# Four FFN ends of a streaming encoder step: the last six inner tiles joined into one output chain, and a final norm in two halves of the tokens

## The chip, the cores and the metric

The program runs on one core of a Trainium2 chip. The metric is the time of one execution on the device in microseconds (us), and a kernel's time is the median of its runs. A product below is one matmul instruction of TensorE on a 128 x 128 weight block and 288 columns, unless said otherwise.

## What is computed

One inference step of a two-layer encoder (each layer: FFN, mixer of MLA and RWKV heads, cross-attention, FFN), on 512 new frames of one stream and 64 of another, 576 tokens in all, with D_MODEL 1024 and D_FF 2816. The change touches the four FFNs and the final norm:

```python
def rmsnorm(x, g):
    xf = x.astype(jnp.float32)
    y = xf * lax.rsqrt(jnp.mean(xf * xf, axis=-1, keepdims=True) + EPS)
    return (y * g.astype(jnp.float32)).astype(x.dtype)

def swiglu_half(x, g, w_gate, w_up, w_down):
    h = rmsnorm(x, g)
    return x + 0.5 * ((jax.nn.silu(h @ w_gate) * (h @ w_up)) @ w_down)
...
    x = swiglu_half(x, lp['ffn1_norm'], lp['ffn1_w_gate'], lp['ffn1_w_up'], lp['ffn1_w_down'])
    y, c_kv, k_r, wkv, shift = token_mixer(rmsnorm(x, lp['mix_norm']), ...)
    x = x + y
    x = mem_attend(x, mk, mv, lp)
    x = swiglu_half(x, lp['ffn2_norm'], lp['ffn2_w_gate'], lp['ffn2_w_up'], lp['ffn2_w_down'])
...
    y_prompt = rmsnorm(xp, final_norm)
    y_sample = rmsnorm(xs, final_norm)
```

The outputs are y of both streams and the updated caches and states.

## The kernel before

**Layout.** x stays in SBUF for the whole step, as eight tiles x[0..7] of 128 features by 576 tokens. The tokens are worked on in two halves of 288 (`hs`, HT). Every operand of a product is held as two parts, a high part and a low part in fp32r, and one weight block times one activation half is three products: high by high (line L315), low activation (L316), low weight (L317), all in `mm3`. The parts are made by `split`: ScalarE copies the high part (L247), VectorE subtracts it (L248). Weights come by DMA from the SP queue into wraw or sraw buffers and are split into whi/wlo or sh/sl buffers, 128 x 512 (four blocks) at a time, a few ahead of their use (`take`, `factors`).

**An FFN** (`ffn`). The 22 inner tiles are eleven pairs. Pairs 0 and 1 are computed plainly. For pairs 2 to 10 the gate and the up of two tiles by two halves are formed by seven products of sums in place of eight (`products`, `sums`): each gate or up is 84 product instructions. The up result is multiplied by the gate, split, and put into the tags xnh and xnl, rings of eight buffers each (`up`). `outputs` multiplies the inner tiles of one or two pairs with the down weights: for each x tile and half, one accumulator takes all products of the tiles, and VectorE adds half of it into x (L521). The loop over pairs 2 to 10 runs up of pair p, gate of pair p+1, and after pairs 3, 5, 7 and 9 the outputs of the last two pairs (wds weights, 192 products). After pair 10 its outputs alone remain (wd weights, 96 products). The list `order` in `ffn` names the weight blocks in the order of use.

**The next norm** (`Norm`) is made while the outputs end. For every x tile ScalarE makes the high part of gain times x (L370), VectorE the low part (L371), again in the xnh and xnl rings; ScalarE squares the tile (L376) and VectorE adds it to a running sum nacc (L378). The first products of the next stage read the high and low parts without the norm's factor. The factor comes later from one fp32 matmul a half on the sum (L386), which is four instructions (passes) in the trace, and `rsqrt`: three ScalarE steps (L300) and two VectorE corrections (L349, L350).

**The final norm** (`final`). Behind the last FFN's second four output tiles, for each half: eight squares on ScalarE, of which two pairs are added for the whole width beforehand, six fp32 matmuls with the ones matrix in one accumulator (L1411, twelve passes for each half), `rsqrt`, then eight scalings, six on VectorE (L1415) and two on GpSimd (L1417), and four DMAs of y (L1419). The first half's norm stands behind the first halves of x[4..7], the second half's behind the second halves.

**What sets the order.** A scheduler puts the instructions of each engine in one queue when the program is built, and the buffers of a tag are taken in turn: an instruction that writes a buffer waits until the last reader of what stood in it is done. Each engine runs its queue in order.

Of the kernel before, what the change touches and what calls it, by code (L numbers as in the profile page):

```python
# [132 lines left out]
def build(tc, I, O):  # L133
# [266 lines left out]
    def ffn(l, which, V, aside=iter(()), final=None, given=()):  # L400
# [28 lines left out]
        for p in pairs:  # L429
# [3 lines left out]
            if (p - PLAIN) % 2:  # L433
                order += [[wds[l, (p - PLAIN) // 2, m]] for m in range(4)]
        order += [[wd[l, PLAIN, g]] for g in range(2)]
# [93 lines left out]


# [66 lines left out]
        def up(g):  # L597
            acts = [(st([128, T], "xnh", F32R), st([128, T], "xnl", F32R)) for f in range(2)]
# [20 lines left out]
        for p in pairs:  # L619
# [3 lines left out]
            acts += up(g)  # L623
            if not end:
                g = gate()
            if (p - PLAIN) % 2:
                all_outputs(acts)
                acts = []
        if final is None:
            all_outputs(acts)  # L630
        else:
            all_outputs(acts, range(4))
            half_done, done = final()
            outputs(acts, range(4, 8), half_done)
            done()
# [753 lines left out]
    def final():  # L1389

        r, sq = st([128, T], "rstd"), st([128, T], "rs")
        y, qs = ([st([128, 2, HT], "s") for _ in range(8)] for _ in range(2))
        qs = [t.rearrange("p a b -> p (a b)") for t in qs]
        for k in range(4):
            ACT.activation(out=qs[k], in_=x[k], func=AF.Square)
            if k % 2:
                (DVE if k == 1 else POOL).tensor_tensor(out=qs[k], in0=qs[k - 1], in1=qs[k], op=ALU.add)

        def out(k, a):
            return y[2 * (k // 2) + a][:, k % 2]  # L1400

        for k in range(2):
            for a in range(2):
                ACT.activation(out=out(k, a), in_=x[k][:, hs[a]], func=AF.Copy, scale=V("fin", k))

        def tail(a):
            ss, s = ps1("b")[:, 0:HT], hs[a]
            for k in (1, 3, 4, 6, 5, 7):
                if k > 3:
                    ACT.activation(out=qs[k][:, s], in_=x[k][:, s], func=AF.Square)  # L1410
                PE.matmul(ss, ones, qs[k][:, s], start=k == 1, stop=k == 7)  # L1411
            rsqrt(ss, 1.0 / D, EPS, r[:, s], sq[:, s])
            for k in (0, 4, 5, 1, 6, 7, 2, 3):
                if k > 1:
                    DVE.scalar_tensor_tensor(out=out(k, a), in0=x[k][:, s], scalar=V("fin", k), in1=r[:, s], op0=ALU.mult, op1=ALU.mult)  # L1415
                else:
                    POOL.tensor_tensor(out=out(k, a), in0=out(k, a), in1=r[:, s], op=ALU.mult)  # L1417
                if k % 2:
# [109 lines left out]
```

## Time and profile before

| | before |
|---|---|
| median of 3 runs | 2820.01 us (2819.73 to 2820.59) |
| profiled execution | 2819.02 us, its span 2817.0 us |
| granted TensorE clock, mean over the span | 0.991 of full speed |
| TensorE matmul | 2733.7 us, 97% |
| TensorE weight load (beside it) | 2629.8 us, 93% |
| VectorE | 2124.5 us, 75% |
| ScalarE | 1351.2 us, 48% |
| GpSimd | 100.1 us, 4% |

The four places at which an FFN ends lie at about 397 to 425 us (first FFN of layer 0, the mixer follows), 1393 to 1419 (second FFN of layer 0, the first FFN of layer 1 follows), 1791 to 1823 (the mixer follows) and 2786 to 2817 (the final norm follows). The profile's page gives each engine's busy time and a chain of waits, which is followed back from the last instruction. The timeline of an engine gives each instruction with its start, and in brackets the idle time of the engine just before it and the instruction whose end released it. In names, b and mm and g are accumulators (PSUM), xnh and xnl the high and low parts, whi/sh and wlo/sl the high and low parts of weights.

### The profile page before, as it was taken

The numbers are of one execution on the slowest core, as the hardware profiler recorded it, in microseconds if no ns is written. First come the engines' busy times: TensorE is split into PE (matmuls) and PEld (weight loads), VectorE is DVE, ScalarE is ACT, GpSimd is POOL, SyncE is SP. The second block draws the span as 40 slices with busy tenths as digits, with TensorE's granted clock in tenths as the row PEclk, the third lists the DMA queues.
The fourth block names the chain that finished last, engine by engine and source line by source line (L and its number), as shares of the span: only waits on it lengthen the run. The fifth ranks groups of instructions, "written<-read, shape, count | busy, mean of one in ns | idle before, by whom it ended". The sixth has DMA issues, their size and how long they took to land.

```text
span 2817.0 us, 55885 instructions
## 1 busy us (share of the span) xinstructions
PE 2733.7 (97%) x22284; PEld 2629.8 (93%) x22284; DVE 2124.5 (75%) x4356; ACT 1351.2 (48%) x2781; POOL 100.1 (4%) x197
## 2 busy tenths in 40 slices
PE   8999999979999999999999999998999999999998
PEld 8999999968889899999999999997888899999998
DVE  8888876875676678777788777769666765887776
ACT  5544446355544544444444444554555445444443
POOL 0000001010000000000000000012000000000000
PEclk9999999989999999999999999999999999999999
DMA  5333333652233222222223222346433332222221
GB/s 192 101 111 114 112 124 110 158 142 91 92 119 117 72 97 72 92 93 92 94 71 105 91 90 91 109 105 171 118 98 123 98 117 64 91 91 90 92 93 60
DMA packets 187573, 293.21 MB, mean 104 GB/s; under 512 B 87066, under 2 KB 113050, under 8 KB 187138
## 3 DMA queue, kind: packets, MB, share of 16 engines
q1 hardware_dynamic: 185010, 285.46, 32.3%
q0 software_dynamic: 2304, 4.20, 0.6%
q8 instruction: 175, 2.87, 0.4%
q14 instruction: 84, 0.69, 0.1%
HBM read 250.36 MB, written 41.63 MB: 104 GB/s over the span
## 4 chain that ended last, share of the span: by engine, by line
PE 92%; DVE 4%; ACT 2%; issue 1%; DMA 0%; DVEq 0%; SPq 0%; POOL 0%; ACTq 0%
PE b L315 18%; PE b L316 18%; PE b L317 18%; PE mm L315 4%; PE mm L316 4%; PE mm L317 4%; PE g L315 4%; PE g L316 3%; PE g L317 3%; PE sm L1028 2%; PE pp L1028 2%; PE sc L315 2%; PE pp L1052 1%; PE sc L316 1%; PE sc L317 1%; PE tp L981 1%
## 5 line engine op out<-in xcount | busy, mean ns | idle before, releaser
L247 ACT ACTIVATE whi<-wraw 128x512 fp32r<-128x512 f32 (+1 forms) x493 | 305.4, 623 | 543.5 <-PE b L316 264.9
L248 DVE TENSOR_TENSOR wlo<-wraw,whi 128x512 fp32r<-128x512 f32 (+1 forms) x493 | 333.8, 680 | 117.6 <-ACT whi L247 99.9
L317 PE MATMUL b<-s,wlo 128*128 128x288 f32 x1388 | 408.0, 295 | 0.0
L316 PE MATMUL b<-s,whi 128*128 128x288 f32 x1388 | 406.7, 294 | 0.0
L315 PE MATMUL b<-s,whi 128*128 128x288 f32 x1388 | 405.5, 296 | 0.0
L315 PE MATMUL b<-xnh,whi 128*128 128x288 f32 x1168 | 344.5, 298 | 11.5 <-ACT xnh L370 7.6
L316 PE MATMUL b<-xnl,whi 128*128 128x288 f32 x1168 | 346.2, 297 | 3.4 <-DVE xnl L248 1.8
L317 PE MATMUL b<-xnh,wlo 128*128 128x288 f32 x1168 | 343.6, 296 | 0.0
L521 DVE SCALAR_TENSOR_TENSOR x<-b,x 128x288 f32<-128x288 f32 x448 | 196.8, 455 | 132.0 <-PE b L317 131.7
L316 PEld LDWEIGHTS b<-s,whi 128*128 128x128 f32 x1388 | 261.2, 188 | 0.0
L317 PEld LDWEIGHTS b<-s,wlo 128*128 128x128 f32 x1388 | 261.2, 188 | 0.0
L315 PEld LDWEIGHTS b<-s,whi 128*128 128x128 f32 x1388 | 259.5, 188 | 0.0
L315 PEld LDWEIGHTS b<-xnh,whi 128*128 128x128 f32 x1168 | 219.5, 189 | 13.1 <-ACT xnh L370 7.6
L316 PEld LDWEIGHTS b<-xnl,whi 128*128 128x128 f32 x1168 | 220.3, 189 | 5.7 <-DVE xnl L371 2.9
L316 PE MATMUL b<-s,sh 128*128 128x288 f32 x756 | 224.1, 297 | 0.0
L317 PE MATMUL b<-s,sl 128*128 128x288 f32 x756 | 223.1, 296 | 0.0
L315 PE MATMUL b<-s,sh 128*128 128x288 f32 x756 | 223.0, 296 | 0.0
L317 PEld LDWEIGHTS b<-xnh,wlo 128*128 128x128 f32 x1168 | 220.3, 189 | 0.0
L315 PE MATMUL mm<-xnh,whi 128*128 128x288 f32 x688 | 204.2, 298 | 5.2 <-DVE shp L391 1.8
L316 PE MATMUL mm<-xnl,whi 128*128 128x288 f32 x688 | 205.1, 298 | 1.0 <-DVE xnl L371 0.9
L317 PE MATMUL mm<-xnh,wlo 128*128 128x288 f32 x688 | 204.1, 297 | 0.0
L247 ACT ACTIVATE whi<-S 128x512 fp32r<-128x512 f32 x171 | 107.9, 631 | 165.8 <-PE b L316 161.9
(474 smaller groups left out, 7241.4 us busy)
## 6 DMA issues: line engine op xcount, KB each, us to landing
wraw<-in_wgu SPq DMA_DIRECT2D x131, 512.0 KB
wraw<-in_wds SPq DMA_DIRECT2D x48, 512.0 KB
sraw<-in_wgu SPq DMA_DIRECT2D x45, 512.0 KB
wraw<-in_win SPq DMA_DIRECT2D x36, 512.0 KB
wraw<-in_wd SPq DMA_DIRECT2D x21, 512.0 KB
sraw<-in_wds SPq DMA_DIRECT2D x16, 512.0 KB
wraw<-in_wmk SPq DMA_DIRECT2D x16, 512.0 KB
wraw<-in_wmv SPq DMA_DIRECT2D x16, 512.0 KB
```

The source lines that it names most:

```text
L247: ACT.activation(out=h, in_=src, func=AF.Copy)
L248: by.tensor_tensor(out=lo, in0=src, in1=h.bitcast(F32), op=ALU.subtract)
L315: PE.matmul(out, wh, ah, start=first, stop=False, **kw)
L316: PE.matmul(out, wh, al, start=False, stop=False, **kw)
L317: return PE.matmul(out, wl, ah, start=False, stop=last, **kw)
L521: DVE.scalar_tensor_tensor(out=o, in0=p, scalar=0.5, in1=o, op0=ALU.mult, op1=ALU.add)
L981: PE.transpose(pT[0:n, c0:c0 + nq], pe_[e][0:nq, kt * 128:kt * 128 + n], ident[0:nq, 0:nq])
L1028: PE.matmul(o, *f(p4, e), start=(n == 0 and p4 == 0), stop=(n == len(terms) - 1), skip_group_check=True)
L1052: i = PE.matmul(p[:, p4], bk[half(e), p4], ck[half(e), p4, 0:128], start=True, stop=True)
```

## The change

In every FFN the outputs after pair 9 and those after pair 10 become one block after pair 10, `last_outputs`, run for x[0..3] and x[4..7]. For each x tile and half one accumulator takes 4 x 3 products of pairs 8 and 9 and then 2 x 3 of pair 10: 18 products a chain, sixteen chains. Sixteen additions into x remain where there were 32. The order of the weights follows. The up of pair 8 writes into the tags rr, a and rs in place of xnh and xnl; so eight buffers of xnh and xnl hold pairs 9 and 10, and the next norm takes its buffers from another place of the ring: its tiles 4 to 7 use buffers that pairs 9 and 10 stood in, where before its tiles 6 and 7 used those of pair 10.

In the final norm each half squares its own 288 columns, VectorE adds the first seven squares one on another (L1427 of the new file), and the ones matrix is multiplied with that sum and with the eighth square: two fp32 matmuls, four passes. The first half's matmul is put behind the last product of the chain of x[5], second half. GpSimd is not used: VectorE scales, two tiles at a time for the first four (L1438, 128 x 576) and one at a time for the rest (L1441).

The diff, whole:

```diff
@@ -430,9 +430,10 @@
             order += [[wgu[l, 2 * q + r, i] for r in range(2)] for q, i in [(p, 0)] * (p == PLAIN) + [(p, 1)] + [(p + 1, 0)] * (p + 1 < NF // 2)]
             if p == PLAIN:
                 order[-2:-2] = [[wd[l, p - 1, g]] for g in range(2)]
-            if (p - PLAIN) % 2:
+            if (p - PLAIN) % 2 and p < NF // 2 - 2:
                 order += [[wds[l, (p - PLAIN) // 2, m]] for m in range(4)]
-        order += [[wd[l, PLAIN, g]] for g in range(2)]
+        for g in range(2):
+            order += [[wd[l, PLAIN, g]]] + [[wds[l, (NF // 2 - 2 - PLAIN) // 2, 2 * g + m]] for m in range(2)]
 
         def factors():
 
@@ -526,6 +527,31 @@
             per = 4 // len(acts)
             for m in ms[::per]:
                 outputs(acts, range(m, m + per))
+
+        def last_outputs(g, acts, by_halves=None):
+
+            w2 = [take(0 if by_halves else 2) for _ in range(2)]
+            w4 = []
+
+            def some(i, s):
+                p = ps1("b")[:, 0:HT]
+                for f in range(4):
+                    mm3(p, cols(w4[i], f), [t[:, s] for t in acts[f]], f == 0, False)
+                for f in range(2):
+                    end = mm3(p, cols(w2[i // 2], i % 2 * 2 + f), [t[:, s] for t in acts[4 + f]], False, f == 1)
+                o = x[4 * g + i][:, s]
+                DVE.scalar_tensor_tensor(out=o, in0=p, scalar=0.5, in1=o, op0=ALU.mult, op1=ALU.add)
+                return end
+
+            for i in range(4):
+                w4.append(take(0 if by_halves else (2, 2, 2, 1)[i]))
+                for s in hs[0:1] if by_halves else hs:
+                    some(i, s)
+            if by_halves:
+                for i in range(4):
+                    end = some(i, hs[1])
+                    if i == 1:
+                        by_halves(end)
 
 
         def plain(act):
@@ -594,8 +620,8 @@
                 silu(out=g[f][:, e], in_=t, func=AF.Silu)
             return g
 
-        def up(g):
-            acts = [(st([128, T], "xnh", F32R), st([128, T], "xnl", F32R)) for f in range(2)]
+        def up(g, tags=None):
+            acts = [tuple(st([128, T], t or turn(*tags), F32R) for t in (("xnh", "xnl") if tags is None else (None, None))) for f in range(2)]
             for f, e, t in sums(xs, lambda f, e: tmp()):
                 o = t if f + e else tmp()
                 DVE.tensor_tensor(out=o, in0=t, in1=g[f][:, e], op=ALU.mult)
@@ -620,18 +646,19 @@
             end = p == pairs[-1]
             if (p - PLAIN) % 2 == 0:
                 next(aside, None)
-            acts += up(g)
+
+            acts += up(g, ("rr", "a", "rs") if p == NF // 2 - 3 else None)
             if not end:
                 g = gate()
-            if (p - PLAIN) % 2:
+            if (p - PLAIN) % 2 and p < NF // 2 - 2:
                 all_outputs(acts)
                 acts = []
+        last_outputs(0, acts)
         if final is None:
-            all_outputs(acts)
+            last_outputs(1, acts)
         else:
-            all_outputs(acts, range(4))
             half_done, done = final()
-            outputs(acts, range(4, 8), half_done)
+            last_outputs(1, acts, half_done)
             done()
         ps.close()
         sc.close()
@@ -1389,35 +1416,31 @@
     def final():
 
         r, sq = st([128, T], "rstd"), st([128, T], "rs")
-        y, qs = ([st([128, 2, HT], "s") for _ in range(8)] for _ in range(2))
-        qs = [t.rearrange("p a b -> p (a b)") for t in qs]
-        for k in range(4):
-            ACT.activation(out=qs[k], in_=x[k], func=AF.Square)
-            if k % 2:
-                (DVE if k == 1 else POOL).tensor_tensor(out=qs[k], in0=qs[k - 1], in1=qs[k], op=ALU.add)
-
-        def out(k, a):
-            return y[2 * (k // 2) + a][:, k % 2]
-
-        for k in range(2):
-            for a in range(2):
-                ACT.activation(out=out(k, a), in_=x[k][:, hs[a]], func=AF.Copy, scale=V("fin", k))
-
-        def tail(a):
+        y = [st([128, 2, HT], "s") for _ in range(8)]
+
+        def tail(a, prior=None):
             ss, s = ps1("b")[:, 0:HT], hs[a]
-            for k in (1, 3, 4, 6, 5, 7):
-                if k > 3:
-                    ACT.activation(out=qs[k][:, s], in_=x[k][:, s], func=AF.Square)
-                PE.matmul(ss, ones, qs[k][:, s], start=k == 1, stop=k == 7)
+            qs = [st([128, 2, HT], "s")[:, 0] for _ in range(8)]
+            for k in range(8):
+                ACT.activation(out=qs[k], in_=x[k][:, s], func=AF.Square)
+                if 0 < k < 7:
+                    DVE.tensor_tensor(out=qs[k], in0=qs[k - 1], in1=qs[k], op=ALU.add)
+            i = PE.matmul(ss, ones, qs[6], start=True, stop=False)
+            if prior is not None:
+                after(i, prior)
+            PE.matmul(ss, ones, qs[7], start=False, stop=True)
             rsqrt(ss, 1.0 / D, EPS, r[:, s], sq[:, s])
-            for k in (0, 4, 5, 1, 6, 7, 2, 3):
-                if k > 1:
-                    DVE.scalar_tensor_tensor(out=out(k, a), in0=x[k][:, s], scalar=V("fin", k), in1=r[:, s], op0=ALU.mult, op1=ALU.mult)
+            for j in range(4):
+                t = y[2 * j + a]
+                if j < 2:
+                    for i in range(2):
+                        ACT.activation(out=t[:, i], in_=x[2 * j + i][:, s], func=AF.Copy, scale=V("fin", 2 * j + i))
+                    DVE.tensor_tensor(out=t, in0=t, in1=r[:, s].unsqueeze(1).to_broadcast([128, 2, HT]), op=ALU.mult)
                 else:
-                    POOL.tensor_tensor(out=out(k, a), in0=out(k, a), in1=r[:, s], op=ALU.mult)
-                if k % 2:
-                    SP.dma_start(O["y"][k - 1:k + 1, :, s].rearrange("k p t -> p k t"), y[2 * (k // 2) + a])
-        return [lambda a=a: tail(a) for a in range(2)]
+                    for i in range(2):
+                        DVE.scalar_tensor_tensor(out=t[:, i], in0=x[2 * j + i][:, s], scalar=V("fin", 2 * j + i), in1=r[:, s], op0=ALU.mult, op1=ALU.mult)
+                SP.dma_start(O["y"][2 * j:2 * j + 2, :, s].rearrange("k p t -> p k t"), t)
+        return [lambda prior=None, a=a: tail(a, prior) for a in range(2)]
 
     xn = open_xn()
     load_x()
```

TensorE's order at the end of the second FFN. In the kernel before, s_13385 and s_13636 are operands of the last up (pair 10), and its result is xnh_17396 to xnl_17399, which the chains that follow read first:

```order
L315 MATMUL b_17465<-s_13385,whi_17440 128x288
L316 MATMUL b_17465<-s_13385,whi_17440 128x288
L317 MATMUL b_17465<-s_13385,wlo_17441 128x288
L315 MATMUL b_17465<-s_13636,whi_17440 128x288
L316 MATMUL b_17465<-s_13636,whi_17440 128x288
L317 MATMUL b_17465<-s_13636,wlo_17441 128x288
L315 MATMUL b_17547<-xnh_17396,whi_17461 128x288
L316 MATMUL b_17547<-xnl_17397,whi_17461 128x288
L317 MATMUL b_17547<-xnh_17396,wlo_17462 128x288
```

In the changed kernel rr_16500 to rs_16503 are the result of pair 8, xnh_16800 to xnl_16803 that of pair 9, and xnh_17100 and xnl_17101 a tile of pair 10:

```order
L316 MATMUL b_17169<-s_13604,sh_17144 128x288
L317 MATMUL b_17169<-s_13604,sl_17145 128x288
L316 MATMUL b_17257<-a_16501,whi_17209 128x288
L317 MATMUL b_17257<-rr_16500,wlo_17210 128x288
L315 MATMUL b_17257<-a_16502,whi_17209 128x288
L316 MATMUL b_17257<-rs_16503,whi_17209 128x288
L317 MATMUL b_17257<-a_16502,wlo_17210 128x288
L315 MATMUL b_17257<-xnh_16800,whi_17209 128x288
...
L317 MATMUL b_17257<-xnh_16802,wlo_17210 128x288
L315 MATMUL b_17257<-xnh_17100,whi_17165 128x288
L316 MATMUL b_17257<-xnl_17101,whi_17165 128x288
L317 MATMUL b_17257<-xnh_17100,wlo_17166 128x288
```

Between the last up product and the first reader of pair 10 the products of pairs 8 and 9 now stand; the first of these chains (b_17257) reads pair 10 as its last six.

VectorE's order where the second FFN ends and the next norm is made: L521 (before) and L543 (changed) are additions into x, L371 low parts, L378 the sum of squares, L248 weight splits. In the kernel before, the last x tile is x_10368:

```order
L371 SCALAR_TENSOR_TENSOR xnl_17700<-x_10362,narrow_62,xnh_17699 128x576
L521 SCALAR_TENSOR_TENSOR x_10368<-b_17659,x_10368 128x288
L521 SCALAR_TENSOR_TENSOR x_10368<-b_17667,x_10368 128x288
L378 TENSOR_TENSOR nacc_17715<-nacc_17715,nsq_17723 128x576
L371 SCALAR_TENSOR_TENSOR xnl_17704<-x_10364,narrow_62,xnh_17703 128x576
L248 TENSOR_TENSOR sl_17839<-wraw_17836,sh_17838 128x512
L248 TENSOR_TENSOR sl_17867<-wraw_17836,sh_17866 128x512
L371 SCALAR_TENSOR_TENSOR xnl_17708<-x_10366,narrow_62,xnh_17707 128x576
L378 TENSOR_TENSOR nacc_17715<-nacc_17715,nsq_17726 128x576
L371 SCALAR_TENSOR_TENSOR xnl_17712<-x_10368,narrow_62,xnh_17711 128x576
L378 TENSOR_TENSOR nacc_17715<-nacc_17715,nsq_17729 128x576
L378 TENSOR_TENSOR nacc_17715<-nacc_17715,nsq_17732 128x576
```

In the changed kernel the last x tile is x_10336, and x_10330 is the fifth (tile 4):

```order
L543 SCALAR_TENSOR_TENSOR x_10334<-b_17551,x_10334 128x288
L378 TENSOR_TENSOR nacc_17651<-nacc_17651,nsq_17668 128x576
L543 SCALAR_TENSOR_TENSOR x_10336<-b_17571,x_10336 128x288
L371 SCALAR_TENSOR_TENSOR xnl_17636<-x_10330,narrow_62,xnh_17635 128x576
L543 SCALAR_TENSOR_TENSOR x_10336<-b_17591,x_10336 128x288
L371 SCALAR_TENSOR_TENSOR xnl_17640<-x_10332,narrow_62,xnh_17639 128x576
L248 TENSOR_TENSOR sl_17775<-wraw_17772,sh_17774 128x512
L248 TENSOR_TENSOR sl_17803<-wraw_17772,sh_17802 128x512
L371 SCALAR_TENSOR_TENSOR xnl_17644<-x_10334,narrow_62,xnh_17643 128x576
L248 TENSOR_TENSOR wlo_17717<-wraw_17686,whi_17716 128x512
L371 SCALAR_TENSOR_TENSOR xnl_17648<-x_10336,narrow_62,xnh_17647 128x576
L378 TENSOR_TENSOR nacc_17651<-nacc_17651,nsq_17671 128x576
```

Before, three low parts (tiles 5 to 7) and four sums stood behind the last addition; now four low parts (tiles 4 to 7), the first ahead of it, and one sum.

VectorE's order at the very end. In the kernel before, x_27842 is the last x tile; the two corrections and six scalings of the first half stand behind the last addition:

```order
L521 SCALAR_TENSOR_TENSOR x_27840<-b_35190,x_27840 128x288
L521 SCALAR_TENSOR_TENSOR x_27842<-b_35198,x_27842 128x288
L349 SCALAR_TENSOR_TENSOR rs_35086<-b_35145,rs_35086 128x288
L350 SCALAR_TENSOR_TENSOR rstd_35085<-rs_35086,rstd_35085 128x288
L1415 SCALAR_TENSOR_TENSOR s_35091<-x_27836,narrow_62,rstd_35085 128x288
...
L1415 SCALAR_TENSOR_TENSOR s_35089<-x_27834,narrow_62,rstd_35085 128x288
L349 SCALAR_TENSOR_TENSOR rs_35086<-b_35206,rs_35086 128x288
L350 SCALAR_TENSOR_TENSOR rstd_35085<-rs_35086,rstd_35085 128x288
```

In the changed kernel x_27746 is the last x tile, and s_35078 to s_35083 are the running sum of the second half's squares:

```order
L543 SCALAR_TENSOR_TENSOR x_27744<-b_35036,x_27744 128x288
L349 SCALAR_TENSOR_TENSOR rs_34838<-b_34991,rs_34838 128x288
L350 SCALAR_TENSOR_TENSOR rstd_34837<-rs_34838,rstd_34837 128x288
L1438 TENSOR_TENSOR s_34839<-s_34839,rstd_34837 128x576
L1438 TENSOR_TENSOR s_34841<-s_34841,rstd_34837 128x576
L1441 SCALAR_TENSOR_TENSOR s_34843<-x_27740,narrow_62,rstd_34837 128x288
...
L543 SCALAR_TENSOR_TENSOR x_27746<-b_35056,x_27746 128x288
L1427 TENSOR_TENSOR s_35078<-s_35077,s_35078 128x288
...
L1427 TENSOR_TENSOR s_35083<-s_35082,s_35083 128x288
L349 SCALAR_TENSOR_TENSOR rs_34838<-b_35076,rs_34838 128x288
L350 SCALAR_TENSOR_TENSOR rstd_34837<-rs_34838,rstd_34837 128x288
```

The first half's corrections and its six scalings moved ahead of the last addition, and six additions of squares stand behind it.

## Rows read from the trace of the kernel before

**Rows 1.** The page's chain of waits, share of the span by engine

```profile
PE 92%; DVE 4%; ACT 2%; issue 1%; DMA 0%; DVEq 0%; SPq 0%; POOL 0%; ACTq 0%
```

**Rows 2.** Windows: stretch, length, busy time (instructions) of each engine, PEclk, DMA share, GB/s

```profile
2705.00:2749.40 44.40, 44.40 (x337) 44.40 (x336) 38.17 (x73) 24.01 (x47) 0.00 (x0) 1.00 0.33 106
2775.00:2786.15 11.15, 11.15 (x87) 11.15 (x86) 8.27 (x16) 5.21 (x10) 0.00 (x0) 1.00 0.01 1
```

**Rows 3.** Timeline of TensorE, first FFN's end: start, duration, instruction, [idle before, releaser]

```profile
397.52 0.40 PE L315 MATMUL b<-xnh,sh 128*128 128x288 f32 x1 [0.59 <-ACT xnh L247]
...
398.65 0.40 PE L316 MATMUL b<-xnl,sh 128*128 128x288 f32 x1 [0.73 <-DVE xnl L248]
...
411.43 0.37 PE L315 MATMUL mm<-xnh,whi 128*128 128x288 f32 x1 [0.34 <-DVE x L521]
...
417.89 0.40 PE L316 MATMUL mm<-xnl,whi 128*128 128x288 f32 x1 [0.95 <-DVE xnl L371]
...
421.01 1.24 PE L386 MATMUL g<-nacc,cst 128*128 128x288 f32 x4 [1.41 <-DVE nacc L378]
```

**Rows 4.** The same, second FFN's end, behind the pair of waits

```profile
1409.86 0.40 PE L315 MATMUL b<-xnh,whi 128*128 128x288 f32 x1 [1.21 <-DVE x L521]
...
1414.59 0.40 PE L316 MATMUL b<-xnl,whi 128*128 128x288 f32 x1 [0.34 <-DVE xnl L371]
...
1417.39 1.24 PE L386 MATMUL b<-nacc,cst 128*128 128x288 f32 x4 [1.75 <-DVE nacc L378]
```

**Rows 5.** The same, third FFN's end, behind the pair of waits

```profile
1806.83 0.37 PE L315 MATMUL mm<-xnh,whi 128*128 128x288 f32 x1 [1.43 <-DVE x L521]
...
1822.60 0.38 PE L315 MATMUL mm<-xnh,whi 128*128 128x288 f32 x1 [1.81 <-DVE shp L391]
```

**Rows 6.** The same, fourth FFN's end, the pair of waits

```profile
2787.22 0.40 PE L316 MATMUL b<-xnl,whi 128*128 128x288 f32 x1 [0.38 <-DVE xnl L248]
...
2788.07 0.54 PE L315 MATMUL b<-xnh,whi 128*128 128x288 f32 x2 [0.31 <-ACT xnh L247]
```

**Rows 7.** Timeline of TensorE, VectorE and ScalarE in the final norm

```profile
2803.00 3.07 PE L1411 MATMUL b<-s,cst 128*128 128x288 f32 x12
...
2803.20 0.46 DVE L521 SCALAR_TENSOR_TENSOR x<-b,x 128x288 f32<-128x288 f32 x1 [1.32 <-PE b L317]
...
2806.11 0.50 ACT L300 ACTIVATE rstd<-b,cst 128x288 f32<-128x288 f32 x1 [1.80 <-PE b L1411]
...
2807.12 0.44 ACT L300 ACTIVATE rs<-rstd 128x288 f32<-128x288 f32 x1
...
2808.66 0.44 DVE L349 SCALAR_TENSOR_TENSOR rs<-b,rs 128x288 f32<-128x288 f32 x1
2809.14 0.46 DVE L350 SCALAR_TENSOR_TENSOR rstd<-rs,rstd 128x288 f32<-128x288 f32 x1
2809.64 3.73 DVE L1415 SCALAR_TENSOR_TENSOR s<-x,narrow,rstd 128x288 f32<-128x288 f32 x6
```

**Rows 8.** Groups by form (busy, mean ns | idle before); last row from VectorE's timeline

```profile
L378 DVE TENSOR_TENSOR nacc<-nacc,nsq 128x576 f32<-128x576 f32 x56 | 42.2, 754 | 0.5
...
L371 DVE SCALAR_TENSOR_TENSOR xnl<-x,narrow,xnh 128x576 fp32r<-128x576 f32 x64 | 51.7, 815 | 1.4 <-ACT xnh L370 0.9
...
L248 DVE TENSOR_TENSOR wlo<-wraw,whi 128x512 fp32r<-128x512 f32 x481 | 330.1, 689 | 114.6 <-ACT whi L247 96.9 <-DMA out_mk<-mkv 2.3 <-issue 0.3
...
1408.99 0.81 DVE L521 SCALAR_TENSOR_TENSOR x<-b,x 128x288 f32<-128x288 f32 x2
```

**Rows 9.** Windows as in rows 2, with TensorE's timeline in the second of them

```profile
2811.00:2817.00 6.00, 0.00 (x0) 0.00 (x0) 2.37 (x5) 0.00 (x0) 0.77 (x1) 0.50 0.57 197
...
576.00:580.00 4.00, 1.75 (x8) 1.43 (x7) 3.55 (x8) 1.87 (x5) 1.45 (x2) 0.50 1.04 247
...
576.29 0.44 PE L315 MATMUL g<-ckvh,whi 128*128 128x288 f32 x1
576.53 0.44 PE L316 MATMUL g<-ckvl,whi 128*128 128x288 f32 x1
```

## The prediction

> **What bounds the kernel now.** I read the chain of waits first. TensorE carries 92% of it [rows 1], so an edit is worth what it takes from TensorE's idle time, or from the stretches after TensorE has stopped. Next I read TensorE's own instructions in order of time with the idle time ahead of each, round the ends of the four FFNs. Inside an FFN there is none: the four stretches of 84 products from the up of pair 8 to the gate of pair 10 fill 44.4 us without a gap, 0.132 us a product, with VectorE busy for 38.2 us of them [rows 2]. At an FFN's end the same pattern stands each time. First come two waits on the split of the last pair's up result, because the products that follow read it at once. Then come waits on the next norm, whose high and low parts VectorE has to make from eight x tiles that are finished only 1.6 us apart. The end of the first FFN shows all five [rows 3]: 0.59 + 0.73, then 0.34 + 0.95 + 1.41 us. The second FFN shows the first two again (one pattern in all; together 1.32 and, in the third, 1.31) and 1.21 + 0.34 + 1.75 [rows 4]. The third has besides them 1.43 + 1.81, the last of these because the norm's factor comes late and the third projection finds no free accumulator [rows 5]. The fourth has only the pair, 0.38 + 0.31 [rows 6], and then the final norm. Neither a queue nor a weight's DMA ends a wait of TensorE there.
>
> **The change part by part.** *Joined chains.* The count of products stays: 192 + 96 in two passes become 288 in one. The adds into x fall from 32 to 16 an FFN; VectorE waits for TensorE in that stretch, so their 16 x 0.46 us count for nothing.
>
> *The pair of waits on the up result.* A chain now begins with twelve products on pairs 8 and 9, which are long done; the order shows them ahead of the first that reads pair 10, and products of the neighbouring chains are put in between as well. For the halves split last, some 40 products, 5 us, lie between the last up product and their first reader. The split needs two to three: the two waits were over 1.9 us after the stretch ended (2786.15, where the window of [rows 2] ends, to 2788.07 [rows 6]). I take them as gone: 1.32 + 1.32 + 1.31 + 0.69 us.
>
> *The waits on the next norm.* Each x tile is now final 36 products, 4.75 us, after the one ahead. Per tile VectorE has two adds (0.81 back to back), a low part (0.81), a sum of squares (0.75) and on average 1.5 weight splits (0.69 each [rows 8]): 3.4 us. So it no longer falls behind, and tiles 0 to 3 are ready when the last chain ends. Against it stands a new wait: pair 8 sits in other buffers, so the ring of xnh and xnl has moved on by two, and norm tiles 4 to 7 (before: 6 and 7) take buffers that the last chain still reads. Their high parts can start only in its last 1.2 us, and the order has all four low parts behind it. Counted from the last product: VectorE does four low parts, two or three weight splits and the last sum, 4 x 0.81 + 3 x 0.69 + 0.75 = 6.1, or 5.4 if neighbours overlap as two adds do (0.81 for the two, 0.46 for one [rows 7, 8]): from about 0.5 us before to 5 or 5.5 after. TensorE meanwhile has 24 products (3.2 us) on tiles 0 to 3, reaches the low part of tile 7 after 44 to 51 (5.8 to 6.7 us), and the sum of squares after 48 to 57 (6.4 to 7.5). So each is just in time, by 0.3 to 1.5 us. At the third end the reduction moves from behind 79 products to behind 55, 3.2 us sooner, against a wait of 1.81. I take all these waits as gone: 2.70 + 3.30 + 3.24 us. From below, if tiles 4 to 7 came 2 us later than I count, 1 to 1.5 us of each would stay. If VectorE were level at every step nothing would stay, and a gain beyond the idle time itself is not possible, since the products' number is the same.
>
> *The final norm.* The half-by-half order costs and gives. It gives TensorE eight fp32 passes: before, each half summed six tiles in twelve passes, 3.07 us or 0.25 each [rows 7]; now VectorE adds seven of the eight and four passes remain, so 2.0 us less stand ahead of the last product. With the 0.69 the last product is 2.7 us sooner. Behind it I count from the moment E at which VectorE takes the last product. Before, E is 2803.20 and the end 2817.0: 13.8 us (2803.20 [rows 7] to where [rows 9] end). After: the first half's square waits for a buffer (rs) that the last chain reads until 13 products before its end, so it ends at E-1.3, and its two corrections end at E-0.3. VectorE's order then has the six scalings of the first half ahead of the last add into x: two of 128x576 (a sum's 0.75) and four of 128x288 (0.41, as the adds back to back [rows 8]), so 3.1 us; six of the latter took 3.73 in the old tail [rows 7], but beside GpSimd, which is not used now. So the last add starts at E+2.9, not at E. Six adds, each on the one ahead, follow at the 0.48 at which such a pair runs (2808.66 to 2809.14 [rows 7]): E+6.2. Then four passes 1.1, ScalarE's three steps 1.45 (2806.11 to 2807.56), two corrections 1.0, scaling 3.1, and the writes 3.6 as before (2813.37, where the last scaling ends [rows 7], to 2817.0): E+16.5 with rounding, 2.7 us longer. That would just eat the 2.7.
>
> TensorE's clock makes it worse. In the old tail TensorE stops at 2806.1 (2803.00 + 3.07 [rows 7]), and from 2811.0 on its granted clock is 0.50, the lower of its two levels [rows 9]. In the new tail TensorE stands still for some 6 us ahead of the last four passes, so I expect them at the lower level. Where that level stands elsewhere, a 128x288 product starts 0.24 us after the one ahead [rows 9], against 0.132 [rows 2]; a pass of 0.25 then takes 0.46 to 0.50 and four cost up to 1.0 us more: E+17.5. I take this end, since the fall came at most 5 us after the stop in the old tail. The final part then nets a loss of 1.0, with bounds of 0 and 1.5.
>
> The Trainium skill (page TensorE: Matmul & The Clock Gate, section Why this matters for your kernels) advises against idle gaps between bursts of products because the gate goes back to its lower level, which speaks against this tail. By that rule the sum is the one with the 1.0 us; without it the forecast would be 1 us lower.
>
> **The sum.** 4.02 + 4.62 + 4.55 = 13.2 us gained at three ends, 1.0 lost at the fourth: 12.2. The profiled execution took 2819.0 us, 1.0 under the median of 2820.0, so the same execution should take 2806.8 and the median 2807.8. I say 2808.
>
> **The rivals.** *The waits come back as late tiles.* Norm tiles 4 to 7 wait for the last chain now, and the margin is as little as 0.3 us. If ScalarE's high parts (with two to four weight copies between them) set the pace and each low part trails by half a microsecond, 1 to 2 us stay at each of three ends: 2811 to 2814. For it speaks that both engines do little else but this then; against it the count above, in which the tightest step still fits.
>
> *Slower: the last up stretch starves.* Before, TensorE had 192 output products, 25 us, between the gate and the up of pair 10, in which weights were made ahead; VectorE was busy for only 8.3 of the 11.15 us of that stretch [rows 2]. Now the up follows the gate at once, the fifth such stretch in a row. If its weights had to be made with none ahead, seven splits and four sums at 0.69, 7.6 us, would be waited for at each of four FFNs: 30 lost against 12, about 2838. It decides as soon as five stretches hold more VectorE work than 55.5 us. Against it: four hold 38.2 of 44.4, and another like them makes 48.
>
> *No difference.* The joined ends gain, but half of it stays as waits and the tail loses more than counted, for instance if the first half's scaling and the last six adds run 2 us longer: 2815 to 2822.
>
> *The change not doing what it says* I rule out: the order shows the joined chains, the buffers and the two tails.
>
> **How the numbers follow.** The forecast, 2805 to 2811, gets 0.70; late tiles 0.15; no difference 0.10 (within 0.2%, 2814.4 to 2825.6, about what a measurement of this kernel can tell from no change); starving 0.05. The first two are faster by over 0.2%: 0.85. The range leaves out 2 in 10: from 2805, all waits gone and the clock not fallen with a little more, to 2814, late tiles at each end.
>
> **What would show it.** Right: no idle time of TensorE over 0.3 us from the up of pair 10 to some 14 us into the next stage, at three ends; the last product 2.7 us sooner counted from the up of pair 10; then a gap of about 6 us on TensorE, passes of the final sum 0.48 us apart at a granted clock of 0.5, and a tail of 17.5 us. Wrong: TensorE waiting on low parts of tiles 4 to 7, on the reduction, or on weight splits in the last up stretch; or a final sum that starts elsewhere than E+6.

## The result, and the profile after

The changed kernel takes 2801.86 us in the median (2801.58 to 2802.85, 5 runs) against 2820.01 (2819.15 to 2821.78, 5 runs): a ratio of 0.9935, 95% interval 0.9922 to 0.9949. That is 18.2 us faster, where 12 were forecast, and below the range that I gave (2805 to 2814). Its profiled execution took 2802.59 us with a span of 2800.8, so the two traces compared below differ by 16.2.

The chain of waits of the changed kernel, share of the span by engine, as in [rows 1]:

```profile
PE 94%; DVE 3%; ACT 2%; DMA 1%; issue 0%; SPq 0%; DVEq 0%; POOL 0%; ACTq 0%
```

The windows of the changed kernel (columns as in [rows 2]) over its four FFN ends, each from within the last pairs to the next norm's sum of squares or to the last product:

```profile
316.48:417.70 101.22, 101.22 (x767) 101.22 (x766) 77.80 (x146) 52.49 (x94) 1.16 (x4) 1.00 0.39 126
1360.00:1405.80 45.80, 45.80 (x347) 45.80 (x346) 30.00 (x53) 20.38 (x33) 0.00 (x0) 1.00 0.27 83
1752.00:1799.00 47.00, 47.00 (x356) 47.00 (x355) 30.20 (x53) 20.56 (x32) 1.14 (x2) 1.00 0.37 127
2700.00:2782.50 82.50, 82.50 (x621) 82.29 (x620) 54.06 (x109) 37.93 (x76) 0.00 (x0) 1.00 0.21 65
```

and over the 13 us behind the first and the third, where the waits at 421.01 [rows 3] and 1822.60 [rows 5] lay before:

```profile
417.70:431.20 13.50, 13.45 (x99) 13.01 (x97) 9.14 (x16) 11.18 (x21) 1.52 (x4) 1.00 0.38 122
1799.00:1812.90 13.90, 13.82 (x101) 13.37 (x99) 9.27 (x16) 11.15 (x21) 1.39 (x4) 1.00 0.37 126
```

Busy time equals the stretch in the first four, and lacks 0.05 and 0.08 us in the last two: every wait of [rows 3 to 6] is gone. The first stretch also shows that the last ups do not starve.

How much that gave is read from the same instruction's start in both timelines (an instruction outside the changed part, us; the last column is what the stretch since the row above gained):

| place | before | after | before minus after | gained |
|---|---|---|---|---|
| first FFN, start of the outputs of pairs 6 and 7 | 287.46 | 288.62 | -1.16 | -1.16 |
| mixer of layer 0 (first FFN's end lies between) | 454.15 | 449.56 | 4.59 | 5.75 |
| second FFN, end of the outputs of pairs 4 and 5 | 1241.06 | 1235.44 | 5.62 | 1.03 |
| third FFN, first pair (second FFN's end between) | 1443.49 | 1431.80 | 11.69 | 6.07 |
| the same place in the third FFN | 1639.40 | 1627.71 | 11.69 | 0.00 |
| mixer of layer 1 (third FFN's end between) | 1848.52 | 1831.30 | 17.22 | 5.53 |
| the same place in the fourth FFN | 2634.96 | 2617.78 | 17.18 | -0.04 |
| last product | 2802.86 | 2782.51 | 20.35 | 3.17 |
| end of the span | 2817.0 | 2800.8 | 16.2 | -4.2 |

The three ends gave 5.75 + 6.07 + 5.53 = 17.35 us, where I had counted 13.2. The fourth and the final norm lost 1.0, as I had counted. The -1.16 and the 1.03 lie where the two programs hold the same instructions, and they come and go between traces: the first 50 us run at a mean granted clock of 0.97 in this trace and at 1.00 in that of before, and a second trace of the changed kernel (the run a_again below) is 1.5 us ahead of the first at 49 us, 0.7 us behind it at 106, 1.4 behind it after layer 0's mixer and 2.4 after layer 1's.

### The profile page after: what moved, and what is told of

Same layout as the page of the kernel before. It is cut to its first block, busy times and chain, and to the rows that moved or that the text cites. A ratio compares the mean times of both kernels' runs of the same rounds, so it can differ in the third digit from the quotient of the medians.

```text
span 2800.8 us, 55769 instructions
## 1 busy us (share of the span) xinstructions
PE 2726.7 (97%) x22268; PEld 2626.4 (94%) x22268; DVE 2096.3 (75%) x4303; ACT 1354.6 (48%) x2789; POOL 95.3 (3%) x192
## 4 chain that ended last, share of the span: by engine, by line
PE 94%; DVE 3%; ACT 2%; DMA 1%; issue 0%; SPq 0%; DVEq 0%; POOL 0%; ACTq 0%
PE b L317 18%; PE b L315 18%; PE b L316 18%; PE mm L315 4%; PE mm L316 4%; PE mm L317 4%; PE g L315 4%; PE g L316 3%; PE g L317 3%; PE sm L1055 2%; PE pp L1055 2%; PE sc L315 2%; PE pp L1079 1%; PE sc L317 1%; PE sc L316 1%; PE tp L1008 1%
## 5 line engine op out<-in xcount | busy, mean ns | idle before, releaser
L248 DVE TENSOR_TENSOR wlo<-wraw,whi 128x512 fp32r<-128x512 f32 (+1 forms) x497 | 336.2, 680 | 124.7 <-ACT whi L247 107.3
L316 PE MATMUL b<-s,whi 128*128 128x288 f32 x1376 | 402.4, 293 | 0.0
L315 PE MATMUL b<-s,whi 128*128 128x288 f32 x1376 | 400.8, 295 | 0.0
L315 PE MATMUL b<-xnh,whi 128*128 128x288 f32 x1128 | 333.9, 297 | 8.8 <-ACT xnh L370 7.5
L316 PE MATMUL b<-xnl,whi 128*128 128x288 f32 x1128 | 333.7, 296 | 1.5 <-DVE xnl L371 1.5
L317 PE MATMUL b<-xnh,wlo 128*128 128x288 f32 x1128 | 331.9, 295 | 0.0
L316 PEld LDWEIGHTS b<-s,whi 128*128 128x128 f32 x1376 | 258.4, 188 | 0.0
L315 PEld LDWEIGHTS b<-s,whi 128*128 128x128 f32 x1376 | 256.5, 188 | 0.0
L316 PE MATMUL b<-s,sh 128*128 128x288 f32 x768 | 227.3, 296 | 0.0
L315 PE MATMUL b<-s,sh 128*128 128x288 f32 x768 | 226.2, 295 | 0.0
L315 PEld LDWEIGHTS b<-xnh,whi 128*128 128x128 f32 x1128 | 212.5, 189 | 9.7 <-ACT xnh L370 7.8
L316 PEld LDWEIGHTS b<-xnl,whi 128*128 128x128 f32 x1128 | 212.9, 189 | 2.9 <-DVE xnl L371 2.6
L317 PEld LDWEIGHTS b<-xnh,wlo 128*128 128x128 f32 x1128 | 212.6, 189 | 0.0
L522 DVE SCALAR_TENSOR_TENSOR x<-b,x 128x288 f32<-128x288 f32 x320 | 139.0, 455 | 84.0 <-PE b L317 84.0
```

The lines of the kernel that those rows point to most:

```text
L248: by.tensor_tensor(out=lo, in0=src, in1=h.bitcast(F32), op=ALU.subtract)
L315: PE.matmul(out, wh, ah, start=first, stop=False, **kw)
L316: PE.matmul(out, wh, al, start=False, stop=False, **kw)
L317: return PE.matmul(out, wl, ah, start=False, stop=last, **kw)
L522: DVE.scalar_tensor_tensor(out=o, in0=p, scalar=0.5, in1=o, op0=ALU.mult, op1=ALU.add)
```

## Where the extra 4 us lie: what a wait costs

Two products on either side of the first two waits of [rows 3], from TensorE's timeline of the kernel before:

```profile
396.50 0.29 PE L316 MATMUL b<-xnl,sh 128*128 128x288 f32 x1
396.63 0.29 PE L317 MATMUL b<-xnh,sl 128*128 128x288 f32 x1
...
398.89 0.29 PE L317 MATMUL b<-xnh,sl 128*128 128x288 f32 x1
```

In a full stream one product starts 0.13 us after the other and lasts 0.29, so two or three overlap. The wait at 397.52 is given as 0.59 us of idle time, but that is counted from the end of the product ahead (396.63 + 0.29; the profile models the ends of products, so the starts are the safer figures). From start to start it is 0.89, 0.76 more than the stream's 0.13. And behind the wait at 398.65 the next start comes after 0.24 us instead of 0.13. So a wait costs its idle time and some 0.27 us more: 0.16 for the overlap that is lost ahead of it, 0.11 for the stream's slow start behind it. The 14 waits of the first three ends ([rows 3 to 5] and two more pairs) have 13.2 us of idle time, and the table gives 17.35 for their going: 0.30 a wait on top, of which 0.27 is read here and the rest (0.4 us for all 14) stays open. **Theory A** is this price. **Theory B** is the idle time alone, with the rest of the gain elsewhere: in the fewer chains and additions (theory C), or in the new final norm (rival N).

## The experiments

All were compared with runs of the kernel before on the same chip (medians 2819.3 to 2819.7). The changed kernel was run again on the chip of the runs on the ring and the tail (2802.98); for the other runs the stretches between equal instructions of the traces say more than the distance of a median from 2801.86.

**Joined chains with the old norm.** The changed kernel, with the final norm of the kernel before, its first matmul put behind the same product (in part):

```diff
-        y = [st([128, 2, HT], "s") for _ in range(8)]
+        y, qs = ([st([128, 2, HT], "s") for _ in range(8)] for _ in range(2))
...
+                i = PE.matmul(ss, ones, qs[k][:, s], start=k == 1, stop=k == 7)
+                if k == 1 and prior is not None:
+                    after(i, prior)
```

> Joined chains as in the changed kernel, but the final norm of the kernel before. Theory A (a wait of TensorE costs the whole delay from start to start, that is its idle time and about 0.27 us more, so the joined chains alone gave some 17.3 us at three FFN ends and 1.24 at the fourth, and the new final norm loses 4.2 behind the last product against 1.9 gained ahead of it): 2.3 us faster than the changed kernel, 2799.6. Rival N (the unexplained 6 us come from the new final norm, and the joined chains gave the 11.9 us of idle time that I counted): 2806 to 2808, slower than the changed kernel.

2799.34 us (2797.44 to 2800.55), ratio 0.9928 (0.9913 to 0.9942). Theory A's number, and rival N's is out: the joined chains carry the whole gain, and the new final norm takes some 2.5 us of it away. By the traces it gives 1.9 us ahead of the last product and loses 5.3 behind it (the tail is 12.7 us here, 18.0 in the changed kernel). In its trace all three ends stand as in the changed kernel, within 0.02 us.

**The new norm alone**, on the outputs of the kernel before (in part, as a diff against the kernel before):

```diff
-        y, qs = ([st([128, 2, HT], "s") for _ in range(8)] for _ in range(2))
+        y = [st([128, 2, HT], "s") for _ in range(8)]
...
+                    DVE.tensor_tensor(out=qs[k], in0=qs[k - 1], in1=qs[k], op=ALU.add)
...
```

> The outputs of the kernel before, with the new final norm alone. Theory A: 1.9 us sooner at the last product and 4.2 us longer behind it, so 2.3 us slower than the kernel before, 2822.3. Rival N (the new norm carries the unexplained 6 us): 2814 or so.

2824.15 us (2822.44 to 2826.95, 10 runs), ratio 1.0017 (1.0008 to 1.0026): slower by 4.5, twice what I expected. Of the 1.9 us ahead of the last product only 0.7 came, since the first half's matmul now waited 0.92 us for VectorE's sums, and the tail behind it grew from 13.8 to 19.3. Rival N is out here too.

**The pair of waits brought back.** One edit in the chains of the changed kernel:

```diff
+                for f in range(2):
+                    mm3(p, cols(w2[i // 2], i % 2 * 2 + f), [t[:, s] for t in acts[4 + f]], f == 0, False)
                 for f in range(4):
-                    mm3(p, cols(w4[i], f), [t[:, s] for t in acts[f]], f == 0, False)
-                for f in range(2):
-                    end = mm3(p, cols(w2[i // 2], i % 2 * 2 + f), [t[:, s] for t in acts[4 + f]], False, f == 1)
+                    end = mm3(p, cols(w4[i], f), [t[:, s] for t in acts[f]], False, f == 3)
```

> The changed kernel, but each chain of 18 begins with its six products on pair 10 and ends with the twelve on pairs 8 and 9; nothing else differs. The pair of waits on the split of the last up result should come back at all four ends. Theory A (start to start: 0.76 + 1.00 + 0.11 us at each of three ends, 1.24 at the fourth): 6.8 us slower than the changed kernel, 2808.7. Theory B (a wait costs its idle time as the timeline gives it, 1.32 + 1.32 + 1.31 + 0.69): 4.6 us slower, 2806.5. Theory C (fewer, longer chains run faster, whatever they read first): no change, 2801.9.

2811.55 us (2808.79 to 2814.88, 6 runs), ratio 0.9969 (0.9958 to 0.9981). The first and the fourth end, TensorE's timeline:

```profile
373.59 0.40 PE L315 MATMUL b<-xnh,whi 128*128 128x288 f32 x1 [0.60 <-ACT xnh L247]
374.82 0.40 PE L316 MATMUL b<-xnl,whi 128*128 128x288 f32 x1 [0.83 <-DVE xnl L248]
375.06 0.29 PE L317 MATMUL b<-xnh,wlo 128*128 128x288 f32 x1
...
2748.34 0.40 PE L315 MATMUL b<-xnh,whi 128*128 128x288 f32 x1 [0.58 <-ACT xnh L247]
2749.47 0.40 PE L316 MATMUL b<-xnl,whi 128*128 128x288 f32 x1 [0.73 <-DVE xnl L248]
```

The pair is back at all four ends, with 1.43 + 1.31 + 1.31 + 1.31 = 5.4 us of idle time. Against the changed kernel, the stretches cost 1.96 + 1.75 + 1.73 + 1.84 = 7.3 us: 0.24 a wait above the idle time. That decides for A, against B and C. The tail behind the last product is 0.7 us longer besides (18.7), so the trace holds 8.0. The medians differ by more (some 9.7 us): the trace is of the fastest of the six runs, and the two fastest had a mean granted clock of 0.991, the other four (2810.6 to 2814.9) one of 0.988 or 0.989. What lowers it in those stays open.

**Twelve and six apart.** Each chain cut into two, with 32 additions again (in part):

```diff
-                    mm3(p, cols(w4[i], f), [t[:, s] for t in acts[f]], f == 0, False)
+                    mm3(p, cols(w4[i], f), [t[:, s] for t in acts[f]], f == 0, f == 3)
+                DVE.scalar_tensor_tensor(out=o, in0=p, scalar=0.5, in1=o, op0=ALU.mult, op1=ALU.add)
+                p = ps1("b")[:, 0:HT]
...
```

> The changed kernel, but each chain of 18 is cut into one of twelve products (pairs 8 and 9) and one of six (pair 10) with an accumulator and an addition into x each: 32 additions again, the products in nearly the same places. Theory A and B (the gain is the waits that went): no change against the changed kernel, 2801 to 2803. Theory C (the unexplained 4 us at three ends come from the fewer chains and additions): 2806 or more.

2803.29 us (2800.92 to 2804.47), ratio 0.9939 (0.9923 to 0.9956). Its starts stand as the changed kernel's at the three ends, within 0.03 us. Fewer accumulators and additions are worth nothing; theory C is out.

**The ring undone.** Pair 8 in xnh and xnl again:

```diff
-            acts += up(g, ("rr", "a", "rs") if p == NF // 2 - 3 else None)
+            acts += up(g)
```

> The changed kernel with pair 8 put into xnh and xnl again, so six of the eight buffers of each hold what the last chains read, and the next norm's tiles 2 to 7 wait for them in place of tiles 4 to 7. Theory A (four tiles late are just covered by 24 products on tiles 0 to 3, six are not: VectorE makes six low parts at 0.81 us behind the last chain against six products on two tiles): 2 to 3 us of waits at each of three ends, 2808 to 2811. Rival (the buffers play no part, the gain is the chains' order alone): 2801.9.

2801.75 us (2799.39 to 2803.95), ratio 0.9935 (0.9918 to 0.9951), beside 2802.98 for the changed kernel on the same chip: not slower, and my expectation was wrong. Six norm tiles waited for buffers, and TensorE did not wait for them. VectorE's timeline at the second end:

```profile
1405.65 0.81 DVE L371 SCALAR_TENSOR_TENSOR xnl<-x,narrow,xnh 128x576 fp32r<-128x576 f32 x1
1406.38 0.75 DVE L378 TENSOR_TENSOR nacc<-nacc,nsq 128x576 f32<-128x576 f32 x1
```

and TensorE's:

```profile
1407.18 0.99 PE L386 MATMUL b<-nacc,cst 128*128 128x288 f32 x3
```

The sum ends at 1407.13 and is read at 1407.18. In the changed kernel it ends 0.71 us ahead of its reader (1405.10, 1405.81). So that margin fell from 0.7 to 0.05 us, and it was enough: from equal instruction to equal instruction the three ends cost 0.0, 0.1 and 0.0 us more than in the changed kernel. The kernel's end, though, is shorter: its tail is 16.0 us in place of 18.0. The changed kernel keeps pair 8 in rs among other tags, and the square of the first half's factor, which also goes to rs, waits there for the last chain that reads pair 8; here it does not (the runs on the tail below show the same 2.0 us). So the other buffers of pair 8 gained nothing at the three ends and cost 2.0 us at the fourth. The median hardly shows it, because this trace was 1.2 us behind the first one of the changed kernel from stretches in which two traces of one kernel differ as well.

**Late tiles.** At three ends all chains of twelve first, then all of six (in part; the order of the weights follows):

```diff
...
-        last_outputs(0, acts)
         if final is None:
-            last_outputs(1, acts)
+            all_outputs(acts[0:4])
+            all_outputs(acts[4:6])
         else:
+            last_outputs(0, acts)
```

> The changed kernel, but at the first three FFN ends the products stand as chains of twelve (pairs 8 and 9) for all eight x tiles and then chains of six (pair 10) for all eight; so the first reader of pair 10 still comes late, while the x tiles are final 1.6 us apart again, as in the kernel before. The pair of waits on the up result should stay gone, and the waits on the next norm come back. Theory A (start to start, in the kernel before 3.9, 4.3 and 3.7 us at the three ends): 11.9 us slower than the changed kernel at least, 2814 to 2816, since two more norm tiles than before also wait for buffers. Theory B (idle time alone: 2.7, 3.3 and 3.24): 9.2 us slower, 2811. Rival (the norm's waits went because the first reader of pair 10 comes late, not because tiles end 4.75 us apart): 2802.

2807.87 us (2806.6 to 2811.57), ratio 0.9961 (0.9947 to 0.9976): some 5 to 6 us slower than the changed kernel, half of what I expected. The rival (no change) is out. TensorE's waits at the three ends:

```profile
414.42 0.40 PE L316 MATMUL mm<-xnl,whi 128*128 128x288 f32 x1 [0.83 <-DVE xnl L371]
418.27 1.00 PE L386 MATMUL g<-nacc,cst 128*128 128x288 f32 x3 [1.33 <-DVE nacc L378]
...
1403.23 0.40 PE L315 MATMUL b<-xnh,whi 128*128 128x288 f32 x1 [0.37 <-DVE x L526]
1406.56 0.40 PE L316 MATMUL b<-xnl,whi 128*128 128x288 f32 x1 [0.41 <-DVE xnl L371]
1409.69 1.24 PE L386 MATMUL b<-nacc,cst 128*128 128x288 f32 x4 [0.66 <-DVE nacc L378]
...
1800.28 0.40 PE L316 MATMUL mm<-xnl,whi 128*128 128x288 f32 x1 [0.36 <-DVE xnl L371]
1802.41 0.40 PE L316 MATMUL mm<-xnl,whi 128*128 128x288 f32 x1 [0.27 <-DVE xnl L371]
```

Seven waits of 4.23 us idle; the stretches cost 2.68 + 2.25 + 1.16 = 6.1 against the changed kernel, 0.27 a wait above idle: price A again. The waits on the norm, 9.2 us idle in the kernel before, are halved, and the run is not the clean test that I meant: its tiles do not end as in the kernel before. There the additions of the last chains run over the first halves of x[0..3] and only then over their second halves; here each tile gets both halves in turn. ScalarE's first high part at the first end, in the kernel before and in this one:

```profile
403.14 0.78 ACT L370 ACTIVATE xnh<-x,narrow 128x576 fp32r<-128x576 f32 x1 [4.43 <-DVE x L521]
...
398.92 0.78 ACT L370 ACTIVATE xnh<-x,narrow 128x576 fp32r<-128x576 f32 x1 [1.59 <-DVE x L526]
```

That is 5.6 us behind the start of the first product on pair 10 there (397.52), of which the pair of waits is 1.9, and 1.9 us behind the product in the same place of the queue here (397.04). At the other two ends it is 6.3 us there and 1.9 here. So the norm began sooner in a run in which the pair of waits was gone and the order of the chains was another; no run parts the two. What the run does show is that a late first reader of pair 10 is not enough: with tiles that end closer together than in the changed kernel, 6.1 us of waits on the norm came back.

**The tail.** The changed kernel once more, and two edits of its final norm:

> The changed kernel once more, as the base for the three that run with it on the same chip: 2801 to 2803 if nothing but the chip differs. In its trace TensorE's starts should stand as in the first trace of it, but for the first 50 us and the mixers' recurrence, where two traces of the same instructions already differ by up to 1.5 us.

> The changed kernel with one name changed: the square of the first half's factor goes to a buffer of the tag nsq, not rs, so it no longer waits for the last chain that reads pair 8. Theory A (that wait holds the first half's corrections and scalings, and with them the last addition into x, 2.9 us behind the last product, and the squares' sums behind it): the tail after the last product shrinks from 18.0 to some 14.7 us, 3.3 us faster, 2798.5. Rival: the last addition isn't what sets the end, and nothing changes, 2801.9.

> The changed kernel with the final norm's work in another order: the second half's squares and their sum are made tile by tile as the last chains end, the first half's matmul stands behind the first tile's second-half chain, two of its four groups of scalings stand ahead of the last addition and two behind it, and the factor's square uses nsq. Behind the last product: addition 0.46, square 0.44, two passes 0.5 at the full clock, ScalarE 1.45, corrections 1.0, scaling 3.1, writes 3.6: 10.6 us in place of 18.0, so 7.3 us faster than the changed kernel, 2794.6, with the last passes 0.25 us apart. If TensorE's clock has fallen all the same, 0.5 more; if the writes of the first half hold up the last ones, 1 to 2 us more.

The first of them is one name:

```diff
-        r, sq = st([128, T], "rstd"), st([128, T], "rs")
+        r, sq = st([128, T], "rstd"), st([128, T], "nsq")
```

The second splits the norm into parts and calls them between the last chains (in part; NORM0 is 0):

```diff
                 for i in range(4):
                     end = some(i, hs[1])
-                    if i == 1:
-                        by_halves(end)
+                    square(4 + i, 1)
+                    if i == NORM0:
+                        norm(0, end)
+                    if i == 2:
+                        copies(1)
+                        scale(0, (0, 1))
+                norm(1)
+                scale(0, (2, 3))
+                scale(1, range(4))
```

On one chip: the changed kernel 2802.98 (2800.44 to 2805.01), the freed buffer 2800.19 (2799.88 to 2801.78), the new order 2796.53 (2795.53 to 2799.68; ratio 0.9918, 0.9904 to 0.9933). The factor's square in the changed kernel, on ScalarE:

```profile
2781.18 0.45 ACT L300 ACTIVATE rs<-rstd 128x288 f32<-128x288 f32 x1 [2.13 <-PE b L316]
```

the tail behind it on VectorE:

```profile
2781.66 0.46 DVE L349 SCALAR_TENSOR_TENSOR rs<-b,rs 128x288 f32<-128x288 f32 x1 [0.75 <-ACT rs L300]
...
2785.70 0.45 DVE L543 SCALAR_TENSOR_TENSOR x<-b,x 128x288 f32<-128x288 f32 x1
2786.07 3.27 DVE L1427 TENSOR_TENSOR s<-s 128x288 f32<-128x288 f32 x6
2793.20 0.46 DVE L349 SCALAR_TENSOR_TENSOR rs<-b,rs 128x288 f32<-128x288 f32 x1 [3.86 <-ACT rs L300]
```

on TensorE:

```profile
2789.39 1.33 PE L1428 MATMUL b<-s,cst 128*128 128x288 f32 x2 [6.59 <-DVE s L1427]
2790.51 1.17 PE L1431 MATMUL b<-s,cst 128*128 128x288 f32 x2
```

the freed buffer on VectorE and TensorE:

```profile
2781.88 1.80 DVE L1441 SCALAR_TENSOR_TENSOR s<-x,narrow,rstd 128x288 f32<-128x288 f32 x4
...
2783.97 0.45 DVE L543 SCALAR_TENSOR_TENSOR x<-b,x 128x288 f32<-128x288 f32 x1
...
2787.08 1.33 PE L1428 MATMUL b<-s,cst 128*128 128x288 f32 x2 [4.56 <-DVE s L1427]
```

and the new order on VectorE:

```profile
2783.59 0.46 DVE L544 SCALAR_TENSOR_TENSOR x<-b,x 128x288 f32<-128x288 f32 x1 [0.41 <-PE b L318]
...
2787.05 0.46 DVE L350 SCALAR_TENSOR_TENSOR nsq<-b,nsq 128x288 f32<-128x288 f32 x1 [1.29 <-ACT nsq L301]
```

and on TensorE:

```profile
2784.78 0.75 PE L1445 MATMUL b<-s,cst 128*128 128x288 f32 x2 [0.74 <-ACT s L1436]
```

In the changed kernel the square waits 2.1 us, the last addition stands 2.9 us behind its product (2782.51 + 0.29), and the six sums stand behind it. With the freed buffer the last addition is still 1.45 us behind its product, since the six scalings of the first half and one of the sums stay ahead of it in the queue; the tail is 16.0 us, so the wait was worth 2.0 us and not the 3.3 that I expected. The medians differ by 2.8; the rest lies ahead of the last product. In the new order the last addition starts at once, the first two of the last four passes follow the last product directly, and TensorE waits 0.74 us for the other two, instead of 6.59 for all four. The tail is 11.1 us (2783.59 to 2794.7) in place of 18.0, where 10.6 were expected, and the median is 6.5 us lower, where 7.3 were. This version takes less time than the changed kernel and the kernel before.

## Why the prediction was wrong

**The step that failed** is the price of a wait. I took each at the idle time that the timeline gives, 13.2 us in sum, and wrote that a gain beyond the idle time itself is not possible. It is: the idle time starts at the end of a product that the stream would have overlapped, and the next start behind a wait is late too. The same 14 waits were worth 17.35; the runs with the pair brought back and with late tiles show the same price (0.24 and 0.27 us a wait above idle). That one term is 4.1 of the 6 us by which the forecast missed, and the false bound set the low end of the range. The rest, 1.7 us, lies between the profiled executions and the medians: that of before was 1.0 us under its median, that of the changed kernel 0.7 over its own. That part of the miss is chance.

**Right: which waits go, and why.** The pair goes because pair 10's first reader comes late, and comes back when it is read first. The waits on the norm go, and no new one takes their place. The expected margins (0.3 to 1.5 us) were the right size: 0.71 at the tightest that I read, the sum of squares at the second end. One reading was off without harm: before, the first four x tiles did not end 1.6 us apart as counted but closer together, since their first halves all came ahead of their second ones: at the first end their last additions start at 402.64, 403.31, 403.98 and 405.08.

**Right in sum, by luck in that two errors cancel: the final norm.** The last product came 3.17 us sooner, not 2.7 (the pair of the fourth end was 1.24 from start to start, not 0.69). The tail is 18.0, not 17.5. By steps, from the end E of the last product (2782.80): the last addition at E+2.9 as counted, the last passes at E+6.6 against 6.2, and two pairs of passes in 2.3 us (2789.39 to 2791.68) against 2.1. The window of the changed kernel there, columns as in [rows 2]:

```profile
2789.40:2791.70 2.30, 2.28 (x4) 1.16 (x4) 0.00 (x0) 0.00 (x0) 0.00 (x0) 0.50 0.00 0
```

and that of the new order's last passes:

```profile
2783.50:2786.00 2.50, 1.29 (x5) 0.38 (x3) 2.17 (x5) 1.66 (x5) 0.00 (x0) 1.00 0.21 74
```

After 6.59 us of idle the granted clock is 0.50, the lower of its two levels, and the four passes start 0.64, 0.48 and 0.48 us apart, where I gave 0.48; after 0.74 us of idle it is 1.00. The Trainium skill (page TensorE: Matmul & The Clock Gate, section Why this matters for your kernels) says that long enough idle gaps between bursts of products bring the lower level back; here the trace agrees (0.50 behind the 6.59 us).

**The rivals.** Late tiles: no wait of that kind is in the trace, and even two more tiles late cost no more than 0.2 us at three ends together. Starving: busy time equals the stretch. No difference: the measured ratio excludes it.

## What to carry to other kernels

Price a wait of TensorE from start to start, not by its idle time: subtract the stream's own spacing from the distance between the two starts, and add what the next start is late. For many short waits the difference is large (0.27 us on waits of 0.3 to 1.8). Where a result is split over two engines before it can be read, put products on older data between it and its reader, and let tiles that feed the next norm end farther apart than the next norm takes for one; and look what stands in a queue behind an instruction that waits for a buffer, as the square of the first half's factor did here (2.0 us).

## What I had not expected of the hardware

Two traces of the changed kernel differ by 0.6 us over the mixer of layer 0 and by 1.1 over that of layer 1, and by up to 1.5 us in the first 50 us, where the mean granted clock was 0.97 in seven of the eleven traces and 1.00 in four, while the long streams of products agree to 0.03 us over hundreds of us. So small edits are measured on stretches between equal instructions, not on the whole span.
